# Two convolution pairs in one pass over x, and a last scaling on two engines with two store queues

## The chip, the core and the metric

The kernel runs on one core of a Trainium2 chip. A core has five engines that work in parallel and meet only at semaphores: TensorE (PE in the profile: matrix products, with PEld for the loading of weights into the array), VectorE (DVE), ScalarE (ACT), GpSimd (POOL) and SyncE (SP), which here only issues DMAs. The operands lie in SBUF, the results of products in PSUM, whose banks VectorE or ScalarE must empty before another product can be summed in them. The metric is the device time of one execution in microseconds (us); three runs of the kernel before took 1125.96, 1127.89 and 1129.59 us, with a median of 1127.89.

## The reference, cut to what matters

One layer of a decoder trunk for 288 tokens (256 of a prompt, 8 x 4 of samples), width 2048, all in float32:

```
h = rmsnorm(x, norm1_g)
a, gate, z = split(h @ w_in + b_in)            # 1024 columns each
u = a * sigmoid(gate)                          # with 30 earlier values in front
c = silu(layernorm(depthwise_conv31(u) + conv_b, ln_g, ln_b))
d = window means of z over 2, 4, 8, 16 tokens, less z      # four groups of 256 columns
p = (d @ pool_w) * pool_scale                  # per group
x = x + concat[c, p] @ w_out
f = relu(rmsnorm(x, norm2_g) @ w_ff1) ** 2     # 8192 columns
y = rmsnorm(x + f @ w_ff2, norm_f)
```

The last values of u and z go out as the new state.

## The kernel before, in words

Activations are kept with the channels on the 128 partitions and the 288 tokens along the row, so x is 16 tiles of 128 x 288 (`xT`). Weights come in blocks of 1 MB (1024 rows x 256 columns, `wr`). Each float32 operand of a large product is split in two parts, hi and lo, and a product is three matmuls: hi x hi (L233), hi x lo of the activations (L234), lo of the weights x hi (L235). The hi part of the weights is a copy on ScalarE (`whi`, L213), the lo part a subtraction (`wlo`, L214) on VectorE or GpSimd; the table `SHARE` says how many of eight lo parts go to GpSimd. For x the hi part `hh` is made on ScalarE (L245) and the lo part `hl` on VectorE (L246).

The input projection goes group by group, each with 256 result columns in two PSUM banks: four convolution pairs (a_i, gate_i), then pooling groups and convolution pairs in turn. The pool of such banks (`acc`) has four, so a group can begin when the group before the last has been evacuated. A group is 16 k x 2 banks x 3 = 96 matmuls. RMSNorm's factor `rb` (1 / sqrt of the mean square, per token) is not applied to x but to the result: the evacuations of the banks (`tg` and `ta`, L302 and L303; `tz`, L341, for a pooling group) multiply by `rb`. It is made from the squares of x, which ScalarE and GpSimd compute and GpSimd and VectorE add in two chains (L279, L281, L283, L285), by `rsqrt_rows`: six small matmuls (`pt`, L182) sum over the partitions, short VectorE and ScalarE steps give 1 / sqrt (`st`, L184 to L191), three more put it on a diagonal (`dg`, L194), a matmul spreads it over the partitions (`pr`, L196), and ScalarE copies it to `rb` (L297). This stands behind the matmuls of pair 0.

After its evacuation a pair is gated (`u_all`, L308) and convolved on VectorE: 31 steps per pair (L313, then the taps, L316), in which the running sum lies in PSUM (`pc`) and u in SBUF; for the samples GpSimd multiplies (L319) and VectorE reduces (L321). A scheduler orders the instructions of each engine when the program is built; each engine then runs its own list strictly in order. The convolutions carry a priority that puts them behind all other work that is ready (`later`).

The eight convolved tiles go through a LayerNorm (`mean`, `ssc`, a second `rsqrt_rows`) before the convolution half of the output projection, while the pooling half (L415) is computed. Then come the second half of that projection, the MLP in four chunks, and the last RMSNorm: `rsqrt_rows`, after which VectorE multiplies 16 tiles in six instructions (L481) and SyncE stores each piece (L482).

At the start SyncE issues the loads: the vectors, then x in eight pieces of two tiles, each followed by a quarter of one of the first two weight blocks.

Of the kernel before, what the change touches and what calls it, by code (L numbers as in the profile page):

```python
# [9 lines left out]
F32 = mybir.dt.float32  # L10
F32R = mybir.dt.float32r
AF = mybir.ActivationFunctionType
ALU = mybir.AluOpType
# [27 lines left out]
# groups of two 128-column results of the input projection, in order: a convolution tile's pair  # L41
# (a_i, gate_i), or a pooling group, the widest windows first
# [26 lines left out]
# of 8 lo parts, how many GpSimd computes  # L69
SHARE = {"first": 2, "second": 4, "conv": 7, "pool": 5, "pool_w": 3, "w_out": 6}  # L70

# per-channel vectors, [P, columns]: channel = column * P + partition
# [10 lines left out]
def trunk_kernel(ctx: ExitStack, tc: tile.TileContext, io):  # L83
    """Activations are channel-major: [channel on the partitions, token]. Tokens: the prompt's
    256, then 8 x 4 of the samples. Every float32 operand of a large product is split exactly in
    two float32r parts (12 bits each): w x = wh xh + wh xl + wl xh, in float32 accumulation."""
# [55 lines left out]
    def load(cuts=((0, 8),), x_cuts=()):  # L142
        """The next 1 MB of weights; at the start in pieces, with pieces of x between them"""
        raw = wraw.tile([P, 8, 256], F32, name=nm("wr"), tag="wr")
        src = io["w"][next(blocks)]
        for j, (k0, k1) in enumerate(cuts):
            if j < len(x_cuts):
                a, b = x_cuts[j]
                nc.sync.dma_start(xT[:, a:b, :], io["xT"][:, a:b, :])
            nc.sync.dma_start(raw[:, k0:k1, :], src[:, k0:k1, :])  # L150
# [17 lines left out]
    for j in range(10):  # L168
# [6 lines left out]
    nc.gpsimd.memset(u_all[:, :, 0:CH], 0.0)  # L175

    def rsqrt_rows(parts, scale, after=None):
        """PSUM [P, T], on every partition: 1 / sqrt(scale * sum over parts and partitions + eps)."""
        pt = ms("pt", 3)
        for j in range(3):  # L180
            for n, t in enumerate(parts):
                nc.tensor.matmul(pt[:TB, j : j + 1], t[:, j * TB : (j + 1) * TB], ones[:, 0:1], start=n == 0, stop=n == len(parts) - 1)  # L182
# [40 lines left out]
    def gemm(banks, rhs, m_outer=False):  # L223
        """banks[m] = sum over k of w(k, m)^T rhs[k]; the next group's weights are split meanwhile"""
# [17 lines left out]
    hx = []  # L242
    for k in range(KT):
        hh, hl = act("hh"), act("hl")
        nc.scalar.activation(hh, xT[:, k, :], AF.Copy, scale=v("norm1_g", k))  # L245
# [295 lines left out]
```

## Time and profile before

| what | value |
|---|---|
| median of three runs | 1127.89 us |
| span of the profiled execution, first to last instruction | 1125.9 us |
| device time of that execution | not given apart; the shortest run is 1125.96 us |
| TensorE busy | 1094.4 us, 97% |
| VectorE busy | 677.1 us, 60% |
| ScalarE busy | 468.7 us, 42% |
| GpSimd busy | 188.8 us, 17% |
| DMA | 187.01 MB, 166 GB/s on average |

A row of the timeline has a start and a duration in us, engine, line, operation, what is written and read, sizes, a count, and in brackets the idle time before it with what ended it. A row of the waits has an engine and line, whom it waited for, us in total, how often, and the longest. A row of instruction groups has busy us, mean ns of one, then idle time before. Busy times of pipelined matmuls overlap, so their spacing, not their duration, tells their price. Spans on GpSimd are rough.

### The profile page before, as it was taken

To read this page: it belongs to the slowest core of one execution; us is meant where nothing else is said; L and a number is where in the kernel's file an instruction comes from. 1 tells how busy PE (TensorE), PEld (TensorE's weight loads), DVE (VectorE), ACT (ScalarE), POOL (GpSimd) and SP (SyncE) were. 2 spreads that over 40 slices of the span, in tenths; PEclk is the share of its full clock that TensorE was granted. 3 is DMA by queue.
4 is the path that set the end of the run, shared out by engine and by line. 5 is a ranking of instruction groups with operands and counts; after the bars stand their busy time and mean duration, and the time that the engine had idled before them with its cause. 6 is when DMAs were issued, how large, how long until landed. Compare 5 with 4: busy or idle time off the path is not lost.

```text
span 1125.9 us, 19336 instructions
## 1 busy us (share of the span) xinstructions
PE 1094.4 (97%) x8190; PEld 1089.8 (97%) x8190; DVE 677.1 (60%) x983; ACT 468.7 (42%) x643; POOL 188.8 (17%) x149
## 2 busy tenths in 40 slices
PE   7998898999999999999999999999999999999995
PEld 7998898999999999999999999999999999999995
DVE  7999999788755544445555444455444445555554
ACT  6443345356544433334444333344433334444441
POOL 4789886612200000000000000000000000000000
PEclk9999998989999999999999999999999999999998
DMA  8554438534445444444445454444444454545432
GB/s 298 191 175 164 148 115 222 184 113 166 172 150 177 160 171 167 158 179 154 184 153 183 152 182 156 174 163 167 170 160 178 153 184 151 183 155 175 162 113 84
DMA packets 31910, 187.01 MB, mean 166 GB/s; under 512 B 3408, under 2 KB 7760, under 8 KB 10448
## 3 DMA queue, kind: packets, MB, share of 16 engines
q1 hardware_dynamic: 31824, 185.78, 47.0%
q8 instruction: 64, 1.05, 0.4%
q14 instruction: 22, 0.18, 0.0%
HBM read 181.49 MB, written 4.28 MB: 165 GB/s over the span
## 4 chain that ended last, share of the span: by engine, by line
PE 86%; DVE 9%; POOL 2%; issue 2%; DMA 1%; ACT 0%; SPq 0%; DVEq 0%; POOLq 0%
PE ac L233 29%; PE ac L234 28%; PE ac L235 28%; DVE pc L316 3%; DVE wlo L214 1%; POOL wlo L214 1%; DVE d L354 1%; DVE ssc L397 1%; DVE d L351 1%; DMA xT<-in_xT 1%; POOL s L347 0%; DVE d L359 0%; DVE z_all L283 0%; PE pt L182 0%; DVE xT L481 0%
## 5 line engine op out<-in xcount | busy, mean ns | idle before, releaser
L213 ACT CAST whi<-wr 128x1024 fp32r<-128x1024 f32 (+1 forms) x342 | 355.0, 1040 | 562.8 <-PE ac L234 543.6
L214 DVE TENSOR_TENSOR wlo<-wr,whi 128x1024 fp32r<-128x1024 f32 (+1 forms) x295 | 364.7, 1236 | 371.8 <-ACT whi L213 371.7
L233 PE MATMUL ac<-ah,whi 128*128 128x288 f32 x1024 | 302.7, 296 | 0.0
L233 PE MATMUL ac<-fh,whi 128*128 128x288 f32 x1024 | 302.4, 295 | 0.0
L234 PE MATMUL ac<-al,whi 128*128 128x288 f32 x1024 | 301.2, 294 | 0.0
L234 PE MATMUL ac<-fl,whi 128*128 128x288 f32 x1024 | 301.2, 294 | 0.0
L235 PE MATMUL ac<-fh,wlo 128*128 128x288 f32 x1024 | 299.3, 292 | 0.0
L235 PE MATMUL ac<-ah,wlo 128*128 128x288 f32 x1024 | 298.8, 292 | 0.0
L235 PEld LDWEIGHTS ac<-fh,wlo 128*128 128x128 f32 x1024 | 193.1, 189 | 0.0
L235 PEld LDWEIGHTS ac<-ah,wlo 128*128 128x128 f32 x1024 | 192.9, 188 | 0.0
L234 PEld LDWEIGHTS ac<-fl,whi 128*128 128x128 f32 x1024 | 192.7, 188 | 0.0
L234 PEld LDWEIGHTS ac<-al,whi 128*128 128x128 f32 x1024 | 192.4, 188 | 0.1
L233 PEld LDWEIGHTS ac<-ah,whi 128*128 128x128 f32 x1024 | 192.1, 188 | 0.1
L233 PEld LDWEIGHTS ac<-fh,whi 128*128 128x128 f32 x1024 | 192.0, 188 | 0.0
L233 PE MATMUL ac<-hh,whi 128*128 128x288 f32 x384 | 113.6, 301 | 7.7 <-DVE tg L302 6.6
L214 POOL TENSOR_TENSOR wlo<-wr,whi 128x1024 fp32r<-128x1024 f32 (+1 forms) x47 | 112.3, 2400 | 34.0 <-ACT whi L213 31.4
L234 PE MATMUL ac<-hl,whi 128*128 128x288 f32 x384 | 114.9, 301 | 3.0 <-DVE hl L246 2.9
L235 PE MATMUL ac<-hh,wlo 128*128 128x288 f32 x384 | 114.2, 301 | 1.5 <-DVE wlo L214 1.4
L316 DVE SCALAR_TENSOR_TENSOR pc<-u_all,vec,pc 128x256 f32<-128x256 f32 x232 | 100.1, 479 | 1.3
L233 PEld LDWEIGHTS ac<-hh,whi 128*128 128x128 f32 x384 | 73.3, 193 | 8.4 <-issue 7.0
L234 PEld LDWEIGHTS ac<-hl,whi 128*128 128x128 f32 x384 | 74.3, 194 | 4.1 <-DVE hl L246 4.1
L235 PEld LDWEIGHTS ac<-hh,wlo 128*128 128x128 f32 x384 | 74.1, 194 | 2.3 <-DVE wlo L214 2.2
(115 smaller groups left out, 875.5 us busy)
## 6 DMA issues: line engine op xcount, KB each, us to landing
wr<-in_w SPq DMA_DIRECT2D x167, 1024.0 KB, 4.9
xT<-in_xT SPq DMA_DIRECT2D x8, 288.0 KB, 5.7
wr<-in_w SPq DMA_DIRECT2D x8, 256.0 KB, 5.6
out_u_out<-u_all SPq DMA_DIRECT2D x1, 1208.0 KB, 8.6
out_yT<-xT SPq DMA_DIRECT2D x2, 576.0 KB, 2.9
u_all<-in_hist_c SPq DMA_DIRECT2D x8, 136.0 KB, 5.8
out_z_out<-z_all SPq DMA_DIRECT2D x1, 668.0 KB, 7.4
z_all<-in_hist_p SPq DMA_DIRECT2D x4, 152.0 KB, 4.0
```

The costliest lines, as they stand in the source:

```text
L213: nc.scalar.copy(hi[:, k : k + cut, :], src)
L214: eng.tensor_tensor(lo[:, k : k + cut, :], src, hi[:, k : k + cut, :].bitcast(F32), op=ALU.subtract)
L233: nc.tensor.matmul(b, wh, xh, start=k == 0, stop=False)
L234: nc.tensor.matmul(b, wh, xl, start=False, stop=False)
L235: nc.tensor.matmul(b, wl, xh, start=False, stop=k == n - 1)
L316: nc.vector.scalar_tensor_tensor(out=dst, in0=up[:, w : w + SEQ], scalar=cwv[:, w : w + 1], in1=pc, op0=ALU.mult, op1=ALU.add)
L351: nc.vector.scalar_tensor_tensor(out=d[:, w - 1 : SEQ], in0=s[:, PH + w - 1 : ZO], scalar=1.0 / w, in1=z[:, PH + w - 1 : ZO], op0=ALU.mult ...
L354: nc.vector.scalar_tensor_tensor(out=samples(d[:, SEQ:T], NS), in0=ss[:, :, PH:], scalar=1.0 / w, in1=zs[:, :, PH:], op0=ALU.mult, op1=ALU ...
L397: nc.vector.tensor_tensor(ssc, ssc, q, op=ALU.add)
```

## The change

- *Loads.* x and the blocks of the first **two** pairs (four blocks) come k by k: first two pieces of one tile, then seven of two, each followed by the same rows of both pairs' weights. The fourth block lies in the room of `u_all`, which is not used until then. The vectors come over ScalarE's queue.
- *First pass.* The splits of the first two pairs stand between those of x, all lo parts on VectorE. `first_pairs` runs over k once, with 12 matmuls per k in four banks; then comes `rsqrt_rows`, and then the two evacuations. The first call of `conv_pair` that makes products of its own is that of pair 2.
- *Squares.* GpSimd squares the first four pieces, ScalarE the last four, and GpSimd makes all seven additions in one chain.
- *`rsqrt_rows`.* The order of the six small matmuls is turned: all three of the first part, then all three of the second.
- *End.* `rf` is also copied to SBUF (`rfs`, ScalarE); VectorE scales 12 tiles, GpSimd four; GpSimd's two pieces are stored over ScalarE's queue.
- Twelve warm-up matmuls in place of ten; comments are dropped, so line numbers move.

```diff
-    nc.sync.dma_start(vec[:, 0:CWO], io["vec"][:, 0:CWO])
-    raw0 = load(((0, 2), (2, 4), (4, 6), (6, 8)), ((0, 2), (2, 4), (4, 6), (6, 8)))
-    raw1 = load(((0, 2), (2, 4), (4, 6), (6, 8)), ((8, 10), (10, 12), (12, 14), (14, 16)))
+    nc.scalar.dma_start(vec[:, 0:CWO], io["vec"][:, 0:CWO])
+    raws = [wraw.tile([P, 8, 256], F32, name=nm("wr"), tag="wr") for _ in range(3)]
+    raws.append(u_all[:].rearrange("p k t -> p (k t)")[:, 0:2048].rearrange("p (k c) -> p k c", c=256))
+    order = (0, 2, 1, 3)
+    first = [raws[order[j]] for j in range(4)]
+    sources = [io["w"][next(blocks)] for _ in range(4)]
+    PIECES = ((0, 1), (1, 2), (2, 4), (4, 6), (6, 8), (8, 10), (10, 12), (12, 14), (14, 16))
+    for a, b in PIECES:
+        nc.sync.dma_start(xT[:, a:b, :], io["xT"][:, a:b, :])
+        r, a8, b8 = a // 8, a % 8, (b - 1) % 8 + 1
+        for j in (r, 2 + r):
+            nc.sync.dma_start(first[j][:, a8:b8, :], sources[j][:, a8:b8, :])
...
-        for j in range(3):
-            for n, t in enumerate(parts):
-                nc.tensor.matmul(pt[:TB, j : j + 1], t[:, j * TB : (j + 1) * TB], ones[:, 0:1], start=n == 0, stop=n == len(parts) - 1)
+        for n, t in enumerate(parts):
+            for j in range(3):
+                nc.tensor.matmul(
+                    pt[:TB, j : j + 1], t[:, j * TB : (j + 1) * TB], ones[:, 0:1],
+                    start=n == 0 and j == 0, stop=n == len(parts) - 1, skip_group_check=True,
+                )
...
+    for a, b in PIECES:
+        for k in range(a, b):
+            hh, hl = act("hh"), act("hl")
...
+        for pair in range(2):
+            src = first[a // 8 + 2 * pair][:, a % 8 : (b - 1) % 8 + 1, :]
+            if a % 4 == 0:
+                first_parts[pair, a // 4] = [wspl.tile([P, 4, 256], F32R, name=nm(n), tag=n) for n in ("whi", "wlo")]
+            hi, lo = (t[:, a % 4 : (b - 1) % 4 + 1, :] for t in first_parts[pair, a // 4])
+            nc.scalar.copy(hi, src)
+            nc.vector.tensor_tensor(lo, src, hi.bitcast(F32), op=ALU.subtract)
...
-    tot = [scratch[:, 0], scratch[:, 1]]
-    used = [False, False]
+    tot = scratch[:, 0]
     for q in range(8):
         xq = xT[:, 2 * q : 2 * q + 2, :]
-        a = 0 if q in (0, 2, 4) else 1
-        dst = scratch[:, 2 if a == 0 else 3 + q % 2] if used[a] else tot[a]
-        if a == 0:
+        dst = scratch[:, 1 + q % 4] if q else tot
+        if q < 4:
             nc.gpsimd.tensor_tensor(dst, xq, xq, op=ALU.mult)
         else:
             nc.scalar.activation(dst, xq, AF.Square)
-        if used[a]:
-            (nc.vector if a else nc.gpsimd).tensor_tensor(tot[a], tot[a], dst, op=ALU.add)
-        used[a] = True
-    nc.vector.tensor_tensor(tot[1], tot[1], tot[0], op=ALU.add)
+        if q:
+            nc.gpsimd.tensor_tensor(tot, tot, dst, op=ALU.add)
...
+    def first_pairs():
+        banks = bank2() + bank2()
+        for k, (xh, xl) in enumerate(hx):
+            for m, b in enumerate(banks):
+                wh, wl = (t[:, k % 4, m % 2 * P : (m % 2 + 1) * P] for t in first_parts[m // 2, k // 4])
+                nc.tensor.matmul(b[:, :T], wh, xh, start=k == 0, stop=False)
+                nc.tensor.matmul(b[:, :T], wh, xl, start=False, stop=False)
+                nc.tensor.matmul(b[:, :T], wl, xh, start=False, stop=k == KT - 1)
+        ready.append(next(weights))
+        nc.scalar.copy(rb, rsqrt_rows([tot[:, 0, :], tot[:, 1, :]], 1.0 / D, AF.Sigmoid)[:, :T])
+        nc.gpsimd.memset(z_all[:, :, 0:PH], 0.0)
+        return banks[0:2], banks[2:4]
...
     rf = rsqrt_rows([ssf, qf], 1.0 / D)
-    for k0, n in ((0, 1), (1, 2), (3, 4), (7, 4), (11, 3), (14, 2)):
+    rfs = row("rfs")
+    nc.scalar.copy(rfs, rf[:, :T])
+    for k0, n, eng, by, queue in (
+        (0, 1, nc.vector, rf, nc.sync), (12, 2, nc.gpsimd, rfs, nc.scalar), (1, 3, nc.vector, rf, nc.sync), (4, 4, nc.vector, rf, nc.sync),
+        (14, 2, nc.gpsimd, rfs, nc.scalar), (8, 3, nc.vector, rf, nc.sync), (11, 1, nc.vector, rf, nc.sync),
+    ):
         xk = xT[:, k0 : k0 + n, :]
-        nc.vector.tensor_tensor(xk, xk, rf[:, None, :T].to_broadcast([P, n, T]), op=ALU.mult)
-        nc.sync.dma_start(io["yT"][:, k0 : k0 + n, :], xk)
+        eng.tensor_tensor(xk, xk, by[:, None, :T].to_broadcast([P, n, T]), op=ALU.mult)
+        queue.dma_start(io["yT"][:, k0 : k0 + n, :], xk)
```

More of the change, by code (lines that the diff above doesn't have):

```diff
@@ L66, in weight_blocks @@
                 yield "w_ff2", r, (c, c + P)
-SHARE = {"first": 2, "second": 4, "conv": 7, "pool": 5, "pool_w": 3, "w_out": 6}
+SHARE = {"conv": 7, "pool": 5, "pool_w": 3, "w_out": 6}
 VEC = (("norm1_g", 16), ("b_in", 24), ("conv_b", 8), ("ln_g", 8), ("ln_b", 8), ("pool_scale", 8), ("norm2_g", 16), ("norm_f", 16))
@@ L167, in trunk_kernel @@
     warm = ms("warm")
-    for j in range(10):
+    for j in range(12):
         nc.tensor.matmul(warm[:, 0:P], ones, ones, start=True, stop=True)
@@ L242, in trunk_kernel @@
     hx = []
[L243 to L247 removed]
+    first_parts = {}
+    for a, b in PIECES:
+        for k in range(a, b):
+            hh, hl = act("hh"), act("hl")
+            nc.scalar.activation(hh, xT[:, k, :], AF.Copy, scale=v("norm1_g", k))
+            nc.vector.scalar_tensor_tensor(out=hl, in0=xT[:, k, :], scalar=v("norm1_g", k), in1=f32(hh), op0=ALU.mult, op1=ALU.subtract)
+            hx.append((hh, hl))
+        for pair in range(2):
[5 more added lines that the diff above has]
+            nc.vector.tensor_tensor(lo, src, hi.bitcast(F32), op=ALU.subtract)
+    nc.gpsimd.memset(u_all[:, :, 0:CH], 0.0)
     korder = [2 * g + m for g in GROUPS for m in range(2)]
     def weight_groups():
[L253 to L255 removed]
+        for kind, _ in SEQUENCE[2:]:
+            yield [split(load(), SHARE[kind]) for _ in range(2)]
         getp = split(load(), SHARE["pool_w"])
```

28 lines of the change are left out of this document (9 added, 19 removed).

## The prediction

> **What bounds the kernel now.** I read the page first, then busy time by stretches, then the waits, then the first 45 us of each engine.
>
> ```profile
> span 1125.9 us, 19336 instructions
> ```
> ```profile
> 0.00:36.00 36.00, 29.28 (x168) 26.82 (x169) 29.71 (x40) 21.95 (x40) 16.74 (x32) 0.95 0.85 293
> 36.00:100.00 64.00, 64.00 (x487) 64.00 (x486) 62.51 (x132) 25.63 (x33) 57.35 (x40) 1.00 0.47 166
> 100.00:185.00 85.00, 74.78 (x549) 73.90 (x547) 83.70 (x168) 33.44 (x50) 70.73 (x48) 0.98 0.48 157
> 185.00:236.00 51.00, 48.87 (x346) 48.45 (x346) 44.72 (x88) 23.50 (x35) 30.25 (x17) 0.94 0.52 170
> 236.00:1111.00 875.00, 875.00 (x6631) 874.78 (x6632) 449.33 (x546) 363.04 (x484) 13.69 (x14) 1.00 0.46 162
> ```
> ```profile
> PE ac L233 <- DVE tg L302: 9.8, 3, 3.6
> PE pt L182 <- DVE ssc L397: 2.0, 1, 2.0
> ```
>
> The columns of the stretches are TensorE matmuls, weight loads, VectorE (DVE), ScalarE (ACT), GpSimd (POOL), granted clock, DMA share, GB/s. Three stages stand out. From 236 to 1111 us TensorE is full: 875 us for 6631 matmuls, 0.132 us each; the change leaves this stage alone. From 36 to 185 us it is VectorE that is full: 146.2 of 149 us, with the 240 convolution taps in it. TensorE, busy too, still has to wait three times (9.8 us) for VectorE to empty a PSUM bank (tg) and once (2.0 us) for the LayerNorm's sum. So the time at which the LayerNorm is done, and with it the start of the long stage, is set by VectorE, and VectorE can begin its convolutions only when rb, the tokens' rstd, is there. The first 36 us are thus worth the time of VectorE's first evacuation (tg of pair 0), not the time that TensorE gains.
>
> ```profile
> 35.41 0.46 DVE L302 TENSOR_TENSOR tg<-ac,rb 128x288 f32<-128x288 f32 x1 [0.20 <-ACT rb L297]
> ...
> 44.00 0.46 DVE L302 TENSOR_TENSOR tg<-ac,rb 128x288 f32<-128x288 f32 x1 [0.51 <-PE ac L235]
> ```
>
> Pair 0 is evacuated from 35.41, while TensorE works on pair 1, which ends at 44.0.
>
> **The change, part by part.**
>
> *Two pairs in one pass.* 12 matmuls per k in place of 6, in all four banks of the pool. All 192 matmuls now stand before the six of the rstd (pt) and its broadcast (pr), so the rb chain, until now beside pair 1's matmuls, has nothing beside it: pair 2 needs the banks that only the evacuations free. Hence: when does the pass end, and how long is the chain?
>
> ```profile
> 9.64 1.38 DVE L246 SCALAR_TENSOR_TENSOR hl<-xT,vec,hh 128x288 fp32r<-128x288 f32 x1
> 10.95 1.92 DVE L214 TENSOR_TENSOR wlo<-wr,whi 128x512 fp32r<-128x512 f32 x1
> 12.79 1.40 DVE L246 SCALAR_TENSOR_TENSOR hl<-xT,vec,hh 128x288 fp32r<-128x288 f32 x1
> 14.11 1.97 DVE L283 TENSOR_TENSOR z_all<-z_all 128x576 f32<-128x576 f32 x1
> 16.00 0.50 DVE L246 SCALAR_TENSOR_TENSOR hl<-xT,vec,hh 128x288 fp32r<-128x288 f32 x1
> 16.43 0.68 DVE L214 TENSOR_TENSOR wlo<-wr,whi 128x512 fp32r<-128x512 f32 x1
> 17.04 0.50 DVE L246 SCALAR_TENSOR_TENSOR hl<-xT,vec,hh 128x288 fp32r<-128x288 f32 x1
> ```
> ```profile
> 4.27 1.15 POOL L279 TENSOR_TENSOR z_all<-xT 128x576 f32<-128x576 f32 x1 [2.32 <-DMA xT<-in_xT]
> 9.12 1.59 POOL L279 TENSOR_TENSOR z_all<-xT 128x576 f32<-128x576 f32 x1 [3.70 <-DMA xT<-in_xT]
> 10.79 1.52 POOL L283 TENSOR_TENSOR z_all<-z_all 128x576 f32<-128x576 f32 x1
> 12.39 1.48 POOL L279 TENSOR_TENSOR z_all<-xT 128x576 f32<-128x576 f32 x1
> 13.95 1.51 POOL L283 TENSOR_TENSOR z_all<-z_all 128x576 f32<-128x576 f32 x1
> ```
>
> While GpSimd works through its sums of squares (9.1 to 15.5 us), VectorE gets through just one instruction per GpSimd instruction: starts 1.31, 1.84, 1.32 and 1.89 us apart. With GpSimd idle, hl comes 0.43 and a 512-wide lo 0.61 us apart. Each GpSimd instruction thus costs a waiting VectorE about 1.1 us (1.15 is its length when alone). Before has 4 of them in a row. The change puts 11 on GpSimd (four squares, seven adds) and takes 5 adds from VectorE, but gives it all lo parts of two pairs.
>
> ```profile
> 8.36 0.62 ACT L213 CAST whi<-wr 128x512 fp32r<-128x512 f32 x1
> ```
> ```profile
> 1.05 4.63 PE L169 MATMUL warm<-ones 128*128 128x128 f32 x20 [1.05 <-DVE ones L159]
> 6.79 0.61 PE L233 MATMUL ac<-hh,whi 128*128 128x288 f32 x1 [1.10 <-ACT whi L213]
> ...
> 26.00 1.10 PE L182 MATMUL pt<-ones,z_all 128*96 128x1 f32 x12
> ...
> 34.22 0.72 PE L196 MATMUL pr<-dg,ones 96*128 96x288 f32 x2
> ```
>
> Start: ScalarE casts the second weight piece at 8.36 us; with it 1.17 MB (53 KB of vectors, two pieces of x of 295 KB, two of weights of 262 KB) have landed. In the new order 1.17 MB stand up to and with x of k = 2, 3, too: about 8.4 us. The single-k pieces before it are there in time, because 12 warm-up matmuls at 4.63/10 each hold TensorE until 6.6 (before: first product at 6.79), so the smaller loads give 0.2 us. From there, VectorE up to the last lo of k = 7: 6 hl (2.6) and 6 lo (3.7), with 9 GpSimd instructions between them (9.9), in all 16.2 us, 24.6. ScalarE's squares pace the adds but don't remove them. Between k = 2 and 7 TensorE waits for these lo parts; the last one but one is done at 24.0, and 16 matmuls of k = 6, 7 and 96 of k = 8 to 15 follow at 0.132, in which VectorE (2.1 us per two k, against 3.2 of TensorE) no longer is late: the pass ends at 38.8. Bounds: 33.4 if GpSimd costs nothing (6.6 + 192 x 0.132 + 1.5 for a slow first clock); 40.5 if the clock falls once more in the waits.
>
> Chain: pt 1.1, its scaling 0.2, sqrt 0.24, four small steps 0.8, dg 0.65, pr 0.77, rb 0.42: 4.2 us, each as in the rows below. Two lo parts of 1024 for pair 2 (2.4 us each) start on GpSimd just when the pass frees their buffers, and a small step with two SBUF inputs waits behind them, as here:
>
> ```profile
> 30.94 0.16 DVE L190 SCALAR_TENSOR_TENSOR st<-st,st 96x3 f32<-96x3 f32 x1
> 31.13 2.28 DVE L191 SCALAR_TENSOR_TENSOR st<-st,st 96x3 f32<-96x3 f32 x1
> 33.44 0.63 DVE L194 TENSOR_SCALAR dg<-ident,st 96x96 f32<-96x96 f32 x3
> ```
> ```profile
> 31.00 2.39 POOL L214 TENSOR_TENSOR wlo<-wr,whi 128x1024 fp32r<-128x1024 f32 x1 [1.46 <-ACT whi L213]
> ```
> ```profile
> 34.98 0.40 ACT L297 COPY rb<-pr 128x288 f32<-128x288 f32 x1 [4.05 <-PE pr L196]
> ```
>
> I add 0.8 for the rest of the first and 2.3 for the second: 7.3. The first evacuation then comes at 46.1, 10.7 us later than 35.41 (bounds 37.6 and 47.8: 2.2 and 12.4 later). TensorE idles these 7 us; pair 2 starts at 47, not 44, which costs nothing more, as VectorE is behind anyway.
>
> *What VectorE gets back until the LayerNorm.* Counting instructions in its order from the first evacuation to the LayerNorm's first subtraction: one 1024-wide lo fewer and two adds to xT more (-0.4); 8 fewer taps directly behind a tap of the same chain (a tap behind its own chain starts 0.52 us later, interleaved 0.39: -1.0); three of GpSimd's lo parts are done before, one of which held u_all up by about 2.2 us; VectorE's waits for ScalarE, GpSimd and pair 1 (0.2 + 0.2 + 0.5) go (-0.9). Together -4.5, bounds 0 and -7 (the waits behind GpSimd in this stage will fall otherwise: lo takes 1444 ns here against 1.22 us alone).
>
> ```profile
> L316 DVE SCALAR_TENSOR_TENSOR pc<-u_all,vec,pc 128x256 f32<-128x256 f32 x232 | 100.1, 479 | 1.3
> L214 DVE TENSOR_TENSOR wlo<-wr,whi 128x1024 fp32r<-128x1024 f32 x14 | 20.2, 1444 | 0.8 <-ACT whi L213 0.8
> ```
>
> *The rstd sums part by part.* Only three of six small matmuls now come after the last square. 10 records took 1.02 us; 6 take 0.6. -0.4 at the end and -0.5 at the LayerNorm.
>
> *Last scaling and stores.*
>
> ```profile
> 1112.60 1.02 PE pt L182 x10
> ...
> 1116.33 0.46 DVE xT L481
> ...
> 1117.45 4.16 DVE xT L481 x4
> ```
> ```profile
> out_yT<-xT SPq DMA_DIRECT2D x2, 576.0 KB, 2.9
> ...
> out_yT<-xT SPq DMA_DIRECT2D x1, 144.0 KB, 1.7
> ```
>
> VectorE does 12 of 16 tiles, 1.2 us less, GpSimd four after a copy of rf (0.4): about 2 x 1.2. VectorE, with one input in PSUM, isn't held up, as the taps at 479 ns beside a GpSimd busy 57 of 64 us show. But then the stores count: 2.36 MB from their first issue. At the 405 GB/s that the load stage shows (below) they need 5.8 us, and what now starts sooner gains 0.4. Bounds 0 (the same engines stay full) and -1.2 (all of VectorE's saving). The Trainium skill, "DMA: Bandwidth & Descriptors", section "Issuing engines are not separate DMA queues", says that issues from several engines share the same 16 DMA engines and save only issue time; by it the second queue would bring some 0.3 us at most, an estimate. No run here shows a store on ScalarE's queue.
>
> ```profile
> 10.00:15.00 5.00, 3.87 (x26) 3.41 (x25) 5.00 (x4) 3.68 (x8) 4.76 (x4) 1.00 1.05 405
> ```
>
> Sum: +10.7 - 4.5 - 0.5 - 0.4 - 0.4 = +4.9 us on a span of 1125.9. That span is the profiled execution's; the runs' median is 1127.89, 2.0 above. From the median: 1132.8.
>
> **The rivals.**
>
> *Faster.* GpSimd's sums slip between VectorE's work: the pass ends at 33.4, the chain meets no lo part, first evacuation at 37.6. Then +2.2 - 4.5 - 1.3 = -3.6: 1124.3. For it: GpSimd's add waits for squares, and 10 us of TensorE's waiting in the first 44 us go. Against: one for one in the rows above. It decides below 37.8.
>
> *No change.* Half of the blocking: evacuation near 41, +5.6 - 4.5 - 1.3 = -0.2: 1127.7.
>
> *Nothing comes back.* Evacuation at 47.8 and the stage as long as before: +12.4 - 1.3 = +11.1: 1139.0. [...]
>
> **How the numbers follow.** Chances: my forecast, slower by 1 to 8 us, 0.50; nothing comes back 0.14; no change 0.20; faster 0.16. Measurement tells about 0.3%, 3.4 us. Of the forecast's part some 0.04 lies below that bound: slower 0.60, same 0.24, faster 0.16. The range leaves out half of the faster rival and the upper end of the last: 1125 to 1139; the likeliest case alone 1129 to 1136.
>
> **What would show it.** Right: tg of pair 0 near 46 us; VectorE's lo parts 1.5 to 2 us long beside GpSimd between 8 and 25; TensorE empty for some 7 us after pt; the LayerNorm's pt some 6 us after 235; from there everything parallel to before. Wrong: the first evacuation before 40 us, or a stage from it to the LayerNorm that is shorter by 8 us and more, because then VectorE's order and not its load had set it.

## The result, and the profile after

The changed kernel takes 1140.30 us (median of four runs, 1139.64 to 1140.61). The kernel before took 1126.93 us beside it. The ratio is 1.0119, with a 95% interval of 1.0103 to 1.0136: the change makes the kernel 13.4 us slower. The forecast was 4.9 us slower, 1132.8 us, with a range up to 1139: the sign was right, the size was not.

The page of the profiled execution (1140.42 us device time), then its busy times by stretches, in the columns of the prediction:

```profile
span 1138.6 us, 19380 instructions
```
```profile
0.00:36.00 36.00, 29.86 (x188) 28.82 (x189) 29.60 (x36) 22.17 (x42) 19.82 (x34) 0.91 0.84 283
36.00:100.00 64.00, 58.04 (x423) 57.15 (x422) 56.73 (x123) 24.17 (x32) 49.27 (x36) 0.95 0.46 157
100.00:185.00 85.00, 78.61 (x571) 77.97 (x570) 81.68 (x165) 33.30 (x48) 72.18 (x51) 0.96 0.44 143
185.00:236.00 51.00, 45.87 (x313) 44.95 (x313) 42.63 (x90) 20.45 (x29) 29.08 (x18) 0.90 0.63 191
...
600.00:700.00 100.00, 100.00 (x757) 100.00 (x756) 47.41 (x52) 35.59 (x40) 0.00 (x0) 1.00 0.48 168
```

The last row of the kernel before:

```profile
600.00:700.00 100.00, 100.00 (x763) 100.00 (x762) 46.45 (x50) 34.94 (x36) 0.00 (x0) 1.00 0.47 166
```

The first stretches are what was forecast: TensorE empty for 6 us behind the pass, a fuller GpSimd at the start. The last row was not. In the middle of the MLP TensorE is full in both kernels, at a granted clock of 1.00, and yet does 757 matmuls in 100 us in place of 763.

So I counted by products. Both kernels have 8112 matmuls into the banks `ac`, numbered here from 0 by their start in the trace. The same number is the same place in the work, whatever stands between; 1968 is the MLP's first.

```
product no.     192     768    1152    1392    1584    1968     8111   end of span
before        43.80  123.22  179.40  218.04  250.88  301.62  1111.29   1125.86
after         48.09  133.30  186.68  228.01  256.67  308.35  1123.76   1138.56
later by       4.29   10.08    7.28    9.97    5.79    6.73    12.47     12.70
```

The 12.7 us are three things: 6.73 at the MLP's first product, 5.74 inside the MLP, 0.23 behind the last product. The middle one is no wait. In 59 groups of 96 products (from no. 2400 on) the mean is 12.63 us before (12.59 to 12.67) and 12.72 after (12.69 to 12.75). The MLP takes 809.67 us in the kernel before, e4, e8 and e11 (the experiments follow below) and 815.40 in the changed kernel, e5 to e7, e9 and e10, all within 0.01. The 6.73 us are less firm: in seven more profiles in which nothing ahead of the MLP but a warm-up matmul differs from the changed kernel (e5, e6, e9, e10, e13, e14, e17) it begins at 307.1 to 310.5.

The early stage in the changed kernel, VectorE's timeline in the pass, then in the rstd chain, and GpSimd's: its last sums beside the first of these rows, then its lo parts in the chain:

```profile
12.17 2.23 DVE L264 TENSOR_TENSOR wlo<-wr,whi 128x512 fp32r<-128x512 f32 x2
14.33 3.01 DVE L256 SCALAR_TENSOR_TENSOR hl<-xT,vec,hh 128x288 fp32r<-128x288 f32 x2
17.27 3.72 DVE L264 TENSOR_TENSOR wlo<-wr,whi 128x512 fp32r<-128x512 f32 x2
20.91 3.26 DVE L256 SCALAR_TENSOR_TENSOR hl<-xT,vec,hh 128x288 fp32r<-128x288 f32 x2
24.09 0.68 DVE L264 TENSOR_TENSOR wlo<-wr,whi 128x512 fp32r<-128x512 f32 x1
```
```profile
40.87 0.16 DVE L192 TENSOR_SCALAR st<-pt 96x3 f32<-96x3 f32 x1 [4.92 <-PE pt L187]
...
41.51 1.00 DVE L197 TENSOR_TENSOR st<-st 96x3 f32<-96x3 f32 x1
...
42.73 2.21 DVE L199 SCALAR_TENSOR_TENSOR st<-st,st 96x3 f32<-96x3 f32 x1
...
47.58 0.46 DVE L331 TENSOR_TENSOR tg<-ac,rb 128x288 f32<-128x288 f32 x1 [1.91 <-ACT rb L315]
```
```profile
17.11 6.75 POOL L298 TENSOR_TENSOR z_all<-z_all 128x576 f32<-128x576 f32 x4
...
40.14 2.35 POOL L222 TENSOR_TENSOR wlo<-wr,whi 128x1024 fp32r<-128x1024 f32 x1 [1.93 <-ACT whi L221]
...
42.58 2.34 POOL L222 TENSOR_TENSOR wlo<-wr,whi 128x1024 fp32r<-128x1024 f32 x1
```

Beside GpSimd's sums three of the four lo parts between 12 and 21 us take 1.6 to 1.9 us and the other 0.68, so that VectorE again gets through about one instruction per GpSimd instruction; the first one behind GpSimd's last of that row takes 0.68. Two small steps of the chain wait out GpSimd's two lo parts. The first evacuation comes at 47.58, forecast 46.1.

### The profile page after: what moved, and what is told of

The parts are those of the page before. It is cut to its first block, busy times and chain, and to the rows that moved or that the text cites. A ratio compares the mean times of both kernels' runs of the same rounds, so it can differ in the third digit from the quotient of the medians.

```text
span 1138.6 us, 19380 instructions
## 1 busy us (share of the span) xinstructions
PE 1101.7 (97%) x8194; PEld 1096.2 (96%) x8194; DVE 676.1 (59%) x987; ACT 469.7 (41%) x649; POOL 191.3 (17%) x153
## 4 chain that ended last, share of the span: by engine, by line
PE 83%; DVE 14%; issue 1%; DMA 1%; ACT 0%; SPq 0%; DVEq 0%; ACTq 0%
PE ac L241 27%; PE ac L243 27%; PE ac L242 27%; DVE pc L345 6%; DVE wlo L222 1%; DVE d L380 1%; DMA wr<-in_w 1%; PE ac L313 1%; DVE u_all L337 1%; PE ac L311 1%; PE ac L312 1%; DVE c L350 0%; DVE c L419 0%; DVE ssc L426 0%; DVE dl L391 0%
## 5 line engine op out<-in xcount | busy, mean ns | idle before, releaser
L221 ACT CAST whi<-wr 128x1024 fp32r<-128x1024 f32 x330 | 346.4, 1052 | 583.7 <-PE ac L242 560.2
L222 DVE TENSOR_TENSOR wlo<-wr,whi 128x1024 fp32r<-128x1024 f32 x287 | 354.1, 1234 | 375.7 <-ACT whi L221 375.6
L243 PE MATMUL ac<-ah,wlo 128*128 128x288 f32 x1024 | 302.0, 295 | 0.0
L515 POOL TENSOR_TENSOR xT<-xT,rfs 128x576 f32<-128x576 f32 x2 | 2.8, 1404 | 818.0 <-ACT rfs L509 818.0
L222 POOL TENSOR_TENSOR wlo<-wr,whi 128x1024 fp32r<-128x1024 f32 x43 | 104.3, 2433 | 31.4 <-ACT whi L221 25.5
L241 PE MATMUL ac<-hh,whi 128*128 128x288 f32 x320 | 96.5, 302 | 6.8 <-DVE tz L370 4.4
L345 DVE SCALAR_TENSOR_TENSOR pc<-u_all,vec,pc 128x256 f32<-128x256 f32 x232 | 98.9, 479 | 1.0
L242 PE MATMUL ac<-hl,whi 128*128 128x288 f32 x320 | 95.9, 300 | 0.0
L243 PE MATMUL ac<-hh,wlo 128*128 128x288 f32 x320 | 95.3, 300 | 0.6 <-POOL wlo L222 0.6
L241 PEld LDWEIGHTS ac<-hh,whi 128*128 128x128 f32 x320 | 61.9, 193 | 8.0 <-issue 6.2
L243 PEld LDWEIGHTS ac<-hh,wlo 128*128 128x128 f32 x320 | 61.9, 194 | 0.8 <-POOL wlo L222 0.8
```

The costliest lines, as they stand in the source:

```text
L221: nc.scalar.copy(hi[:, k : k + cut, :], src)
L222: eng.tensor_tensor(lo[:, k : k + cut, :], src, hi[:, k : k + cut, :].bitcast(F32), op=ALU.subtract)
L241: nc.tensor.matmul(b, wh, xh, start=k == 0, stop=False)
L242: nc.tensor.matmul(b, wh, xl, start=False, stop=False)
L243: nc.tensor.matmul(b, wl, xh, start=False, stop=k == n - 1)
L345: nc.vector.scalar_tensor_tensor(out=dst, in0=up[:, w : w + SEQ], scalar=cwv[:, w : w + 1], in1=pc, op0=ALU.mult, op1=ALU.add)
```

## The experiments

All are told against the kernel before in the same job (medians 1125.99 to 1126.89). "MLP" is the start of product 1968, "pace" the mean time of 96 products in the MLP. The changed kernel has 47.58 (first evacuation), 308.35 (MLP), 12.72 (pace).

```
                              median    ratio [95%]              evacuation   MLP     pace
e1 chain early               1133.14   1.0065 [1.0048, 1.0082]     42.14    307.51   12.63
e2 no GpSimd squares         1127.58   1.0008 [0.9999, 1.0018]     36.30    301.21   12.63
e3 both                      1128.41   1.0019 [1.0008, 1.0029]     37.53    302.06   12.63
e4 before, chain late        1126.17   0.9998 [0.9986, 1.0010]     35.52    298.35   12.63
e5 after again               1139.94   1.0118 [1.0103, 1.0133]     47.25    308.27   12.72
e6 after, old tail           1139.79   1.0117 [1.0100, 1.0134]     47.95    308.63   12.72
e7 loads in twos             1141.47   1.0134 [1.0119, 1.0149]     48.86    310.41   12.72
e8 before, new tail          1125.85   0.9996 [0.9987, 1.0006]     35.38    301.30   12.63
e9 after, 2 instr. more      1139.87   1.0122 [1.0106, 1.0139]     46.94    307.12   12.72
e10 after, 4 instr. more     1140.38   1.0128 [1.0113, 1.0143]     48.77    308.89   12.72
e11 before, 2 instr. more    1126.37   1.0000 [0.9991, 1.0009]     35.85    300.59   12.63
e12 e2 + LayerNorm in PSUM   1129.45   1.0025 [1.0011, 1.0040]     37.74    304.47   12.63
e13 after, pr twice          1140.98   1.0124 [1.0108, 1.0140]     49.33    310.52   12.72
e14 after, pr thrice         1140.86   1.0126 [1.0109, 1.0143]     47.40    307.69   12.72
e15 before, pr twice         1128.85   1.0015 [1.0006, 1.0025]     35.87    302.09   12.63
e16 e2, pr twice             1128.12   1.0013 [1.0004, 1.0023]     37.61    302.17   12.63
e17 after, cut near 335 us   1141.29   1.0124 [1.0104, 1.0143]     47.46    308.63   12.72
e18 before, cut near 327 us  1127.26   1.0007 [0.9993, 1.0021]     35.58    300.18   12.63
```

### The first evacuation and what depends on it

**e1.**

```diff
         for k, (xh, xl) in enumerate(hx):
+            if k == 12:
+                nc.scalar.copy(rb, rsqrt_rows([tot[:, 0, :], tot[:, 1, :]], 1.0 / D, AF.Sigmoid)[:, :T])
...
-        nc.scalar.copy(rb, rsqrt_rows([tot[:, 0, :], tot[:, 1, :]], 1.0 / D, AF.Sigmoid)[:, :T])
```

> Edit: the changed kernel, with the rstd chain (six small matmuls, the row scaling, its broadcast) issued inside the merged pass, so that its small matmuls stand ahead of the last 36 products instead of behind all 192. Theory A (the time of VectorE's first evacuation sets the end one for one): the pass ends near 39.7 us as before the edit, the chain lies beside the last products, the first evacuation comes at 41 to 42 instead of 47.6, and the end some 6 us earlier, near 1134. Theory B (VectorE's order after the pass, with its new waits, sets the LayerNorm's time): the first evacuation comes earlier, but the LayerNorm's sum stays within 2 us of 246.6 and the time near 1140.

The evacuation came at 42.14 and the time fell by 7.2 us, to 1133.1: on the face of it theory A with its number. The count by products says otherwise. The MLP began only 0.84 us earlier than in the changed kernel; the rest is the pace, 12.63 in place of 12.72. Of the 5.4 us at the evacuation 3.3 were lost on VectorE by the last tap, as the gating (`u_all`, two SBUF inputs) now fell beside GpSimd's lo parts. VectorE's groups from 35 to 231 us, the changed kernel and then e1:

```profile
L337 DVE SCALAR_TENSOR_TENSOR u_all<-ta,vec,tg 128x256 f32<-128x256 f32 (+1 forms) x16 | 8.0, 543 | 0.0
```
```profile
L338 DVE SCALAR_TENSOR_TENSOR u_all<-ta,vec,tg 128x256 f32<-128x256 f32 (+1 forms) x16 | 11.5, 761 | 0.0
```

Another 1.5 us went between the LayerNorm's sum (pt) and its first use (n): 8.4 us there, 6.9 in the changed kernel. So theory A, one for one, does not hold for the early stage either.

**e2.**

```diff
-        if q < 4:
-            nc.gpsimd.tensor_tensor(dst, xq, xq, op=ALU.mult)
-        else:
-            nc.scalar.activation(dst, xq, AF.Square)
+        nc.scalar.activation(dst, xq, AF.Square)
         if q:
-            nc.gpsimd.tensor_tensor(tot, tot, dst, op=ALU.add)
+            nc.vector.tensor_tensor(tot, tot, dst, op=ALU.add)
```

> Edit: the changed kernel, with all eight squares on ScalarE and the seven adds on VectorE; GpSimd does none of the sums of squares. Theory A (GpSimd's eleven instructions hold VectorE up one for one in the pass): VectorE's lo parts between 10 and 24 us fall from 1.6-1.9 us to 0.7, the adds cost 5 us of VectorE in their place, the pass ends 3 to 6 us earlier than 39.7, and the end of the run moves by the same, to 1134-1137. Theory B (the loads of x and of the weights set the pass): the pass still ends within 1 us of 39.7, and the time stays near 1140.

VectorE's timeline in e2's pass:

```profile
11.14 1.36 DVE L264 TENSOR_TENSOR wlo<-wr,whi 128x512 fp32r<-128x512 f32 x2
...
15.37 0.75 DVE L295 TENSOR_TENSOR z_all<-z_all 128x576 f32<-128x576 f32 x1
...
16.47 1.29 DVE L264 TENSOR_TENSOR wlo<-wr,whi 128x512 fp32r<-128x512 f32 x2
...
36.30 0.46 DVE L328 TENSOR_TENSOR tg<-ac,rb 128x288 f32<-128x288 f32 x1 [2.19 <-ACT rb L312]
```

A lo part takes 0.69 us, an add 0.75, and the last product of the pass starts at 34.58 in place of 39.60: theory A for the pass, and GpSimd's sums were the price of it. With the pass shorter, the scheduler also put the chain inside it (pt at 29.40), so that the evacuation comes 11.3 us earlier. The MLP starts 7.1 us earlier, and the pace is 12.63; these two things, which the edit did not aim at, put the time below theory A's 1134 to 1137. This version is level with the kernel before; it does not beat it.

**e3.** Both edits.

> Edit: both of the edits before this one: the rstd chain inside the pass, and GpSimd without sums of squares. Theory A: the gains add up, the first evacuation comes near 37 us and the end near 1129 to 1130, so level with the kernel before within 0.3%. Theory B (the stage behind the evacuation has become longer by the new order, whatever its start): 1135 or more.

The scheduler had placed the chain as in e2 already, so there was little left to add: 1128.4 and an evacuation at 37.53, near theory A's 1129 to 1130 and 37, far from theory B's 1135. Part of it is again the pace.

**e4.**

```diff
+    first_banks = [bank2(), bank2()]
+    for bk in first_banks:
+        gemm(bk, hx)
+    nc.scalar.copy(rb, rsqrt_rows([tot[1][:, 0, :], tot[1][:, 1, :]], 1.0 / D, AF.Sigmoid)[:, :T])
...
-        if i == 0:
-            nc.scalar.copy(rb, rsqrt_rows([tot[1][:, 0, :], tot[1][:, 1, :]], 1.0 / D, AF.Sigmoid)[:, :T])
```

> Edit: the kernel before, with its own loads, splits, sums of squares and tail, and pair 0 and pair 1 one after the other as before; only the rstd chain is issued behind both pairs' products instead of behind pair 0's. Theory A: pair 1's products end near 44 us, the chain of 4 to 7 us follows, the first evacuation comes at 48.5 to 51 instead of 35.4, and the end 13 to 16 us later, near 1140 to 1143. Theory B (the LayerNorm's time is set by the amount of work and the products, and VectorE catches up): less than half of that delay reaches the end, under 1134.

This says nothing on either theory: the scheduler issued the chain where it was ready, among pair 1's products, so the evacuation stayed at 35.52. The edit did not take place on the chip. Its MLP starts 3.3 us earlier than the kernel before's all the same; that is the granted clock near 240 us, told below.

**e7.**

```diff
-    PIECES = ((0, 1), (1, 2), (2, 4), (4, 6), ...
+    PIECES = ((0, 2), (2, 4), (4, 6), ...
```

> Edit: the changed kernel with the first two loads of one k each joined to one of two, as in the kernel before; all else stays. Theory A (the forecast: the smaller first loads give 0.2 us): the pass ends within 0.7 us of 39.7 and the time stays within 1 us of the changed kernel's in the same job. Theory B (the smaller loads feed TensorE's and VectorE's queues earlier and what follows is chained to that): the pass ends 1.5 us later and more, and the end with it.

The time rose by 1.5 us (four runs from 1140.67 to 1142.59, e5 in the same job 1138.75 to 1140.37), so theory A's bound of 1 us does not hold. In the profile the first product came at 6.20 in place of 5.22 (e5), the pass ended 1.6 us later (last product 40.88, e5 39.27) and the MLP began 2.1 later, as theory B has it. But the eight profiles with the changed kernel's own loads spread as far: first product at 5.15 to 6.30, last of the pass at 38.98 to 41.35. By the times the smaller first loads are worth about 1.5 us, not 0.2; by what way is not shown.

### The pace in the MLP

**e5.** The changed kernel once more.

> The changed kernel once more, not edited. Counted by products (8112 in every kernel), its profile was 6.7 us behind the kernel before at the first product of the MLP, and lost another 5.7 us from there to the last product: 96 products took 12.72 us there, against 12.61 in the kernel before and in the three runs derived from the changed kernel. Theory A (this pace belongs to the program): 12.72 us again and a time near 1140. Theory B (the pace belongs to the executions on that occasion, not to the change): 12.61 us, and a time near 1134.5.

Theory A: 12.72 again, in another job. The pace belongs to the program.

**e9, e10, e11.** The place of TensorE's instructions:

```diff
     for j in range(12):
         nc.tensor.matmul(warm[:, 0:P], ones, ones, start=True, stop=True)
+    half = ones[:].bitcast(mybir.dt.bfloat16)[:, 0:P]
+    nc.tensor.matmul(warm[:, 0:P], half, half, start=True, stop=True)
```

e11 has the same two lines behind the ten warm-ups of the kernel before; e10 has `range(13)` and no other edit.

> Edit: the changed kernel with one more small matmul (bfloat16) behind the warm-ups, which puts two more instructions (a weight load and a matmul) ahead of everything that TensorE does later. So far the pace in the MLP went with the length of TensorE's compiled program: 12.72 us per 96 products in the three programs of 16425 instructions (changed kernel, with the old tail, with loads in twos), 12.63 in those of 16419 (kernel before and its variants) and 16423 (the three others). Theory A (the place of TensorE's instructions, modulo four, sets the pace): 16427 leaves the same remainder as 16423 and 16419, so 12.63, and a time near 1134.3. Theory B (the pace comes from what the changed kernel does in the first 50 us or from the work of the other engines): 12.72 and 1140.

> Edit: the changed kernel with 13 warm-up matmuls instead of 12; in float32 one is four instructions of TensorE (16429, the remainder of the changed kernel). The counterpart of the run before it. Theory A (remainder modulo four): 12.72 as in the changed kernel, 1140 and up to 0.5 more. Theory B (any shift ends the slow pace, or a longer period than four): 12.63, 1134.

> Edit: the kernel before with one more small matmul (bfloat16) behind its ten warm-ups: 16421 instructions; all products keep their order and their addresses. Theory A (remainder modulo four): the pace becomes 12.72 us per 96 products and the time 5 to 6 us longer, near 1131.5, with the first 300 us as in the kernel before. Theory B (the slow pace belongs to the changed kernel): 12.63, 1126.

The 600 to 700 us of e9, then of e11:

```profile
600.00:700.00 100.00, 100.00 (x758) 100.00 (x757) 46.67 (x52) 35.48 (x40) 0.00 (x0) 1.00 0.47 165
```
```profile
600.00:700.00 100.00, 100.00 (x763) 100.00 (x762) 46.75 (x50) 34.12 (x36) 0.00 (x0) 1.00 0.48 167
```

Theory A falls. It had fitted nine programs and failed at the first test: neither shift moved the pace of either kernel.

**e13 to e16.** The starts of the products follow a rhythm. Start to start in ns, six products from the same place each:

```
                     no. 1704, MLP not begun     no. 2076, between pt and pr   no. 2166, behind pr
before               137 126 132 133 132 133     138 126 131 134 132 133       131 134 131 132 132 131
after                134 132 133 137 126 132     133 130 126 131 134 132       138 126 131 134 132 133
```

There are two rhythms, one with steps of 137 and 126 ns (12.70 us per 96) and one without the 137 (12.6). The changed kernel has the long step in the second half of each k, the kernel before in the first; at the small matmuls of the third rstd they go different ways. The edit was to call that rstd's pr two or three times:

```diff
-        nc.tensor.matmul(pr[:, :T], ones[:TB, :], dg[:TB, :], start=True, stop=True)
+        for _ in range(times):
+            nc.tensor.matmul(pr[:, :T], ones[:TB, :], dg[:TB, :], start=True, stop=True)
```

> Edit: the changed kernel, with the broadcast matmul (pr) of the third rstd, near 328 us, issued twice in place of once; nothing else differs in TensorE's order or in the addresses. Up to that place all kernels run their products at 12.70 us per 96; behind its small matmuls (pt near 321 us, pr near 328 us) the changed kernel goes on at 12.72 and the kernel before at 12.63, with two different rhythms of the starts (133, 132, 133, 137, 126, 132 ns against 131, 133, 130, 126, 131, 134). Theory A (TensorE has two steady rhythms, and the place at which the small matmuls cut in decides which one follows): a longer cut changes the phase and can flip it: 12.63 and a time near 1134.5. Theory B (something else in the changed kernel holds the slow pace): 12.72, and the time longer by the extra matmul, some 0.3 us.

> Edit: as the run before it, with pr three times. Theory A: one of the two cuts at least gives 12.63 us per 96 products and a time near 1134.5. Theory B: 12.72 in both, 1140.5.

> Edit: the kernel before with the third rstd's pr issued twice; all else as it was. Theory A: a longer cut can flip its rhythm too, then 12.72 us per 96 products and a time 5.5 to 6 us longer, near 1132. Theory B (the kernel before has no cause of a slow pace): 12.63, within 0.5 us of the kernel before.

> Edit: the version without GpSimd's squares, with the third rstd's pr issued twice. Theory A: if a cut of this length flips the kernel before, it flips this version also, since its rhythm ahead of the cut and behind it was that of the kernel before: 12.72, some 1133. Theory B: 12.63, near 1127.8.

No pace moved: theory B four times on the pace (e15's time, 1128.85, is 2.0 above the kernel before, though, where 0.5 was expected). A longer cut in the same place goes the same way.

**e17, e18.** A cut in a place where none was:

```diff
+            if ch == 0 and g == 1:
+                nc.tensor.matmul(ms("px")[:, :T], ones, r2, start=True, stop=True)
```

> Edit: the changed kernel with one more small matmul (float32, 288 columns, its result unused) between the second and the third group of the MLP's products, near 341 us; no product changes its order or its addresses. In the runs so far the rhythm of the starts changes only where small matmuls cut in, and it then stays: from 200 us on the changed kernel's family has its long step (137, 126 ns) at the second half of each k, the others at the first half; then pt and pr each can change it, and the changed kernel leaves pr in the rhythm of 12.72, the others in that of 12.63; two or three pr in one place count as one cut. Theory A (a cut in another place changes the rhythm once more, and it then stays for the rest of the run): 12.63 us per 96 products from 342 us on, and a time near 1135. Theory B (the rhythm goes back to what belongs to the program): 12.72, and 1140.5.

> Edit: the same one small matmul between the second and the third group of the MLP's products, in the kernel before. Theory A: its rhythm, too, changes there, to 12.72 us per 96 products, and the time is some 6 us longer, near 1132.5. Theory B: 12.63 and a time within 1 us of the kernel before.

Theory B. The cut came at 335.5 us in e17 and 327.1 in e18, between the second group and the third. In e18 it did change the rhythm: behind it the starts go 133, 132, 138, 125, 132, 133, as in the changed kernel, and the group with the cut takes 12.93 us. But by the next group it is back at 12.62, and 12.61 from there. In e17 it stays slow. So the small matmuls can change the rhythm, and at the end of a group it returns to one that belongs to the program.

**What stays open.** What gives a program its pace is not settled. Excluded by runs: the occasion (e5), the old or new tail (e6), the first loads (e7), a shift of TensorE's instructions by two or four (e9 to e11), the length of a cut (e13 to e16) and a new cut (e17, e18). e1 has the same order of products and the same addresses of their operands and banks in the MLP as the changed kernel, and the other pace. Two more things can be ruled out. The length of TensorE's list is not it: e9 has 16427 instructions, and e16, which is 16423 and the four of one more pr, has as many; their paces are 12.72 and 12.63. Nor is the order of the other engines' work: from product 2400 to 8000 VectorE and ScalarE run the same 416 and 370 instructions in the same order in all twenty profiles. All nine profiled runs with 12.72 have the first rstd's chain behind the whole pass, with TensorE empty for 5 us between its pt and pr; all eleven with 12.63 have products between the two. That goes together; no run shows that it is the cause.

### The tail, and the LayerNorm

**e6, e8.** The changed kernel with the lines of the old end, and the kernel before with the new end and the new order of the small matmuls.

> Edit: the changed kernel with the last scaling and the stores of the kernel before (all on VectorE, one queue). Theory A (the new tail is worth nothing): the time from the last product to the end of the run is 14 to 14.6 us with either tail, and the times differ by under 1 us. Theory B (the forecast's 0.8 us, which something in the profiled run hid): with the old tail it is 0.5 to 1 us longer than with the new one. The pace of the products, 12.61 or 12.72 us per 96, is told by the run before this one, as the products are the same.

> Edit: the kernel before with the change's last scaling and stores (VectorE and GpSimd, two queues) and its order of the rstd's six small matmuls, the early stage as before. Theory A (tail worth nothing): the time from the last product to the end stays within 0.4 us of the kernel before's 14.3 us, the time level with it. Theory B (the forecast): 0.8 us shorter at the end, 0.5 us at the LayerNorm, 1125.

Theory A in both. From the start of the last product to the end of the span it is 14.58 us in the kernel before and 14.29 with the new end (e8); in the changed kernel 14.81, with the old end 14.67 (e6). e8 shows the parts: the last pt comes 0.34 us earlier (the order of the small matmuls, forecast 0.4); the first multiply comes 0.87 us behind pr's second half in place of 0.45, since ScalarE's copy `rfs` is now ahead of it; and the last store is issued 1.4 us earlier, at 1120.26, but lands after 4.04 us in place of 3.11, so that from the first multiply to the last landing only 0.25 is gained (8.20, before 8.45). This agrees with the Trainium skill ("DMA: Bandwidth & Descriptors", section "Issuing engines are not separate DMA queues"), which states that DMAs started by several engines run on the same 16 DMA engines.

**e12.** e2, and in the LayerNorm:

```diff
-    nc.scalar.mul(mean, pmean[:, :T], 1.0 / DC)
+    ssp = cvp.tile([P, T], F32, name="ssp", tag="cv", padded_shape=[P, 512])
...
-        nc.vector.tensor_tensor(cs[i], cs[i], mean, op=ALU.subtract)
+        nc.vector.scalar_tensor_tensor(out=cs[i], in0=pmean[:, :T], scalar=-1.0 / DC, in1=cs[i], op0=ALU.mult, op1=ALU.add)
...
-                nc.vector.tensor_tensor(ssc, ssc, q, op=ALU.add)
+                nc.vector.tensor_tensor(ssc if i == N8 - 2 else ssp, ssp, q, op=ALU.add)
```

> Edit: the version without GpSimd's squares, and in the LayerNorm the mean is subtracted from PSUM directly (no copy by ScalarE) and the squares are summed in PSUM, so that these small VectorE instructions have only one input in SBUF. Theory A (a VectorE instruction with two SBUF inputs waits out GpSimd's lo part; one with an input in PSUM does not): the first subtraction, 1.71 us in that version, and the long ssc add, 2.49, fall to about 0.45, the copy's 0.8 goes, the LayerNorm's pt comes some 4 us earlier than 238.6 and the end with it, near 1123.5 at a pace of 12.63 (this program's length leaves a remainder not seen so far, so the pace is open). Theory B (TensorE's own products set the time from there): the first product of the MLP moves by less than 1 us.

VectorE's groups from 222 to 247 us in e2, then in e12:

```profile
L423 DVE TENSOR_TENSOR ssc<-ssc,q 128x288 f32<-128x288 f32 x6 | 4.8, 792 | 0.2
L416 DVE TENSOR_TENSOR c<-c,mean 128x288 f32<-128x288 f32 x8 | 4.3, 606 | 1.5 <-ACT mean L413 1.5
```
```profile
L415 DVE SCALAR_TENSOR_TENSOR c<-pmean,c 128x288 f32<-128x288 f32 x8 | 3.0, 450 | 1.1 <-PE pmean L411 1.1
L422 DVE TENSOR_TENSOR ssp<-ssp,q 128x288 f32<-128x288 f32 x5 | 2.3, 462 | 0.2
```

Theory A on the instructions: with one input in PSUM each takes 450 or 462 ns beside the same lo parts of GpSimd. This agrees with the Trainium skill ("SBUF — State Buffer", section "Who interferes with whom"), by which a VectorE instruction with at most one SBUF input does not contend with GpSimd. Not on the time: the last sum is done at 236.6, but its pt stands behind pooling products in TensorE's list and starts at 239.4. From the evacuation to pt it is 201.6 us, 202.3 in e2. The evacuation itself came 1.4 us later than in e2, the MLP 3.3 later, and the time is 1129.45, where theory A had 1123.5. A gain on VectorE there goes into a wait for TensorE's place in the list.

## Why the prediction was right or wrong, point by point

- *A, the pass (forecast to end at 38.8).* Its last product starts at 39.6. GpSimd blocks VectorE one for one, as the rows above and e2 show: right, 0.8 short. The 0.2 us for the smaller first loads was too little by e7's time (1.5).
- *B, the chain (7.3 us).* From pt at 39.73 to the evacuation at 47.58 it took 7.85: right. 12.2 us later than before, forecast 10.7.
- *C, "what VectorE gets back until the LayerNorm" (-4.5): failed.* From the first evacuation to the last tap it is 183.3 us in both kernels, with 364 and 365 VectorE instructions. The taps did get 1.2 us cheaper (their row goes from 100.1 to 98.9 us; forecast 1.0) and the small e products are no longer held up, but the waits behind GpSimd moved to other instructions. VectorE's groups from 35 to 231 us, before and after:

```profile
L354 DVE SCALAR_TENSOR_TENSOR d<-s,z_all 128x32 f32<-128x32 f32 x8 | 8.5, 1063 | 0.0
L351 DVE SCALAR_TENSOR_TENSOR d<-s,z_all 128x241 f32<-128x241 f32 (+3 forms) x8 | 6.8, 854 | 0.2 <-POOL s L347 0.2
...
L362 DVE TENSOR_TENSOR dl<-d,dh 128x288 fp32r<-128x288 f32 x8 | 3.6, 451 | 0.2
L358 DVE TENSOR_TENSOR e<-s,rcnt 128x15 f32<-128x15 f32 (+3 forms) x8 | 3.4, 426 | 0.0
```
```profile
L222 DVE TENSOR_TENSOR wlo<-wr,whi 128x1024 fp32r<-128x1024 f32 x14 | 19.5, 1392 | 3.4 <-ACT whi L221 3.4
L380 DVE SCALAR_TENSOR_TENSOR d<-s,z_all 128x241 f32<-128x241 f32 (+3 forms) x8 | 12.2, 1527 | 0.0
...
L391 DVE TENSOR_TENSOR dl<-d,dh 128x288 fp32r<-128x288 f32 x8 | 5.9, 736 | 0.0
L383 DVE SCALAR_TENSOR_TENSOR d<-s,z_all 128x32 f32<-128x32 f32 x8 | 5.0, 628 | 0.0
...
L387 DVE TENSOR_TENSOR e<-s,rcnt 128x15 f32<-128x15 f32 (+3 forms) x8 | 1.2, 154 | 0.0
```

  -3.5 (L354 and L383) and -2.2 (e) stand against +5.4 (L351 and L380) and +2.3 (dl), and VectorE waits 3.4 us for ScalarE's hi parts where it waited 0.8; the one lo part fewer (21.4 to 19.5 us in all) and smaller rows make up the rest. What holds up whom is dealt anew by the scheduler; I had counted only the holds that went.
- *The LayerNorm's pt (6 us after 235).* It came 11.3 later, at 246.58; but the MLP starts only 6.73 later. 4.5 us came back behind pt, where "everything parallel" was forecast. Products 1392 to 1584 take 28.7 us, 32.8 before. 1.0 us of the difference is a shorter wait: TensorE was itself 10 us late by product 1392 and waited 1.0 us for the LayerNorm's sum, 2.0 before. The other 3.1 us go with the clock, not with less work or waiting: behind that wait the granted clock of the kernel before falls to 0.50. e4, with the same products and the same wait of 2.0 us, keeps 1.00 and takes 29.7 us for them. The kernel before and e4:

```profile
235.50:242.30 6.80, 6.80 (x34) 6.80 (x34) 4.28 (x12) 2.74 (x4) 0.00 (x0) 0.50 0.45 154
```
```profile
235.50:242.30 6.80, 6.80 (x55) 6.69 (x55) 5.35 (x15) 3.77 (x6) 0.00 (x0) 1.00 0.45 154
```

  The clock falls there in the kernel before, e8, e11, e15 and e18, but not in e4; in the nine profiles of the changed kernel and its variants with a pace of 12.72 it falls near that place in two (e13, e17). No run shows what decides it.

  So the sum up to the MLP (+10.7 - 4.5 - 0.5 = +5.7, measured +6.73) was near for reasons that were not the one given, one of them the clock.
- *D and E, the end (-0.8): failed by size.* +0.23 measured. The small matmuls gave their 0.34; scaling and stores lay within their bounds (0 to -1.2) at -0.25, and the copy that now stands ahead of the first multiply costs 0.42 (all three by e8, which ends 0.29 earlier in sum). The changed kernel's end is 0.5 us longer than e8's, and that goes with the clock: its granted clock falls to 0.50 before pr (1127.67), the kernel before's and e8's behind it, so pr's halves start 0.64 us apart in place of 0.35, and the first multiply comes 1.15 us behind the second half in place of 0.87. The kernel before and the changed kernel at pr:

```profile
1115.50:1116.10 0.60, 0.56 (x2) 0.30 (x2) 0.00 (x0) 0.00 (x0) 0.00 (x0) 1.00 0.00 0
```
```profile
1127.70:1128.30 0.60, 0.60 (x1) 0.46 (x2) 0.00 (x0) 0.00 (x0) 0.00 (x0) 0.50 0.00 0
```

- *"From 236 to 1111 us TensorE is full: the change leaves this stage alone" was the step that failed most.* The matmuls are the same, 0.132 us each by that row; but they come every 131.5 ns before and every 132.5 after, 5.74 us over the MLP. The trace of the kernel before could have given the bound: its products come at 12.70 us per 96 in most stretches without a wait up to 320 us, and at 12.63 behind. An open 0.7% on 800 us belonged into the range.
- *The rivals.* "Nothing comes back" (1139.0, chance 0.14) has the nearest time and the right statement on VectorE's stage; but 4.5 us did come back later (3.1 of them with the clock), and the 5.7 us of the pace, which no rival had, made up for them. Two of its errors cancel.

## What to carry to other kernels

Compare two versions by the start of the same numbered product, not only by the time: e1 gave the time that its theory forecast, and for another reason. A hold of VectorE behind GpSimd is not saved when the instruction that suffered from it is moved: count who stands beside GpSimd's work in the new order, or give the instruction an input in PSUM, as e12 does (which shortened the instructions, but not the time). Before a difference is put down to waits, look at the granted clock of both stretches. And where one engine is full for 800 us, its pace is a term of the sum, with a range, even if the change does not touch a line there.

## What the runs showed of the hardware

- The same products in the same order, at the same addresses (the changed kernel and e1), at a granted clock of 1.00, run at 12.72 or 12.63 us per 96, within 0.05 us in all groups; the changed kernel, profiled twice, had 12.72 both times. The cause is open.
- With one VectorE input in PSUM a subtraction beside GpSimd's lo parts takes 450 ns where that with two SBUF inputs takes 606 on average, the held ones 1.3 to 2 us more (e2: a subtraction of 1.71 and a sum of 2.49 us).
- TensorE's products come at half their pace where its granted clock is 0.50 (0.24 us apart from 237.5 to 242 in the kernel before, else 0.13), and the length of a wait alone does not decide whether it falls: behind the same 2.0 us before the LayerNorm's pt it is 0.50 in the kernel before and 1.00 in e4, pt's matmuls start 0.16 and 0.085 us apart, and 6.8 us hold 34 and 55 matmuls.
- At the end of the run pr's two halves start 0.35 us apart in the five profiles in which the granted clock falls 0.4 us or more behind the first half (before, e2, e8, e11, e16), and 0.58 to 0.64 apart in the fifteen in which it falls ahead of it or within 0.1 us of it.
